# Dense experts: eight tiles per PSUM sum, splits of 1024 columns, two tiles per gelu and gate product, gathers in the output-only stretch

## The chip, the core and the metric

The kernel runs on one core of one Trainium2 chip. The metric is the device time of one execution in microseconds (us). TensorE does the matrix products, VectorE and ScalarE the elementwise work, GpSimd issues the indirect loads (gathers), and SyncE's queue (SP) issues nearly all other transfers; all transfers share 16 DMA engines. In the rows PE is TensorE, PEld its weight load, DVE VectorE, ACT ScalarE, POOL GpSimd, SP SyncE.

## The reference, cut to what matters

One encoder layer on 512 tokens of width 2048. Two mixers (retention, dilated attention) and a projection give x; the change touches only what follows, the PEER layer:

```
h2 = rms_norm(x); q = h2 @ w_query
for each token, 8 heads: top 16 of 16384 experts by two sub-key scores (e1, e2); gates = softmax
a   = h2 . u[expert]                       # 128 chosen experts per token
out = sum over them of gelu(a) * gate * v[expert]
x   = x + out
```

u and v are (16384, 2048) in float32.

## The kernel before, in words

Products keep float32 accuracy by splitting each operand into a high part (a cast on ScalarE) and a low part (a subtraction on VectorE); each product is three matmuls: high x high, high x low, low x high.

The 512 tokens are four blocks of 128. Blocks 0 and 1 are **gathered**: per block (a `Unit`) 128 rows of u, then 128 rows of v are fetched, one row for each token at a time, by an indirect DMA on GpSimd (`gather_issue`, L752), and used on VectorE (`gather_use`, L761 and L770). Three row buffers turn. `tick(anchor, rate)` adds `rate` to a credit; for each whole credit it uses the oldest row if more than two wait, and issues the next gather; its VectorE work is queued behind `anchor`. Block 0's gathers run under the second mixer; block 1's 256 gathers run under the dense experts.

Blocks 2 and 3 (256 tokens, `ND`) are **dense**: all 16384 experts in 128 tiles of 128. For a tile, `expert_in` (L848 to L850, 48 matmuls of 256 columns) makes a = u h2 in PSUM (`psa`), gelu goes to `ge` (L853); `load_u` loads the next tile of u, 1 MB, and splits it in four pieces of 512 columns (L836, L837). The weights of the gates are built earlier as a dense table GD by one-hot products (L906 to L915): in 32 steps of 8 tokens VectorE compares, ScalarE scales by the gate, TensorE multiplies. `weigh` multiplies `ge` by the table (L937) and splits the product (L940, L941). `expert_out` takes v in pieces of two tiles x 512 columns (L955, split at L958 and L959) and sums NV = 4 tiles in PSUM (`psy`, L965 to L967, 24 matmuls of 512 columns a tile), then adds the sum to `yacc` in SBUF (L970), with one tick behind each addition.

In time: 24 tiles of `expert_in` run ahead, 11 while the routing is done and most of the others between the one-hot steps, which carry a tick of 1.2 each. Then come the groups: group g weighs its tiles and runs `expert_in` for those from 24 on, and `expert_out` of group g-1. So there are some groups with output alone and no tick, then 25 groups with both and 8 ticks each, which spread what is left of the 256 gathers evenly, and a last group of output alone with no tick. The compiler's scheduler fixes each engine's order from program order and its own costs; on each engine and each queue that order is then kept. SP's queue holds the loads of u, v and the gate table in one order.

## Time and profile before

| | us |
|---|---|
| time, median of 3 runs | 4723.65 (4723.06 to 4727.6) |
| profiled execution, its own time | 4720.41 |
| its span | 4718.6 |
| TensorE busy in the span | 4278.5 |
| VectorE busy | 3560.2 |
| ScalarE busy | 1999.0 |
| GpSimd busy | 746.5 |

The profiled execution's time is 1.8 us more than its span. A busy matmul is one in the pipeline, so a share of 100% doesn't say that TensorE is at its peak: there the distance between two starts is read. A VectorE operation's duration overlaps the next one's a little: there, too, the distance between starts is what it costs in a row.

### The profile page before, as it was taken

How to read it: one execution, taken by the hardware profiler on the slowest of the kernel's cores; microseconds unless marked ns; L12 is line 12 of the kernel's file. 1: busy time of each engine (PE TensorE's matmuls, PEld its weight loads, DVE VectorE, ACT ScalarE, POOL GpSimd, SP SyncE). 2: the span in 40 equal slices, each digit the busy share in tenths (PEclk: the TensorE clock that was granted, in tenths of full speed). 3: DMA queues.
4: the chain of work that ended last, by engine and by line, in shares of the span. 5: the costliest groups of instructions: out<-in, count | busy, mean ns of one | idle time of the engine just before them, and what ended most of it. 6: DMA issues, size and time to landing. Idle time of an engine off the chain costs nothing.

```text
span 4718.6 us, 58782 instructions
## 1 busy us (share of the span) xinstructions
PE 4278.5 (91%) x21606; PEld 3567.6 (76%) x21606; DVE 3560.2 (75%) x5039; ACT 1999.0 (42%) x3154; POOL 746.5 (16%) x516
## 2 busy tenths in 40 slices
PE   8999989988989999889879987877999999999998
PEld 6888767765767877677668866876788888888887
DVE  7454645546667788577578869887789999999998
ACT  5444545545433333433432332465444434344343
POOL 0000000000001222122122210032012222244232
PEclk9999999999999999899889988988999999999999
DMA  7667666668668889689599873488789999999998
GB/s 242 221 220 232 210 219 205 224 229 274 205 214 301 328 306 342 217 324 336 192 376 388 342 301 136 143 308 341 235 304 364 360 372 369 379 363 362 359 374 300
DMA packets 491744, 1358.81 MB, mean 288 GB/s; under 512 B 47168, under 2 KB 127040, under 8 KB 405952
## 3 DMA queue, kind: packets, MB, share of 16 engines
q1 hardware_dynamic: 414368, 815.99, 49.5%
q0 software_dynamic: 73728, 536.90, 29.7%
q8 instruction: 169, 2.77, 0.2%
q10 hardware_dynamic: 3360, 2.17, 0.1%
q14 instruction: 119, 0.97, 0.1%
HBM read 1290.05 MB, written 64.88 MB: 287 GB/s over the span
## 4 chain that ended last, share of the span: by engine, by line
PE 49%; issue 17%; DMA 15%; DVE 11%; ACT 4%; POOL 3%; SPq 0%; POOLq 0%; ACTq 0%; DVEq 0%
PE gB L146 11%; PE gB L147 10%; PE gB L145 10%; POOL gr L752 3%; PE psy L966 3%; DMA gr<-in_peer_v,eid 3%; DMA wraw<-in_w_in 3%; PE psy L967 3%; PE psy L965 2%; DVE wlo L130 2%; ACT whi L129 2%; PE psa L848 2%; PE psa L850 2%; PE psa L849 2%; DMA vr<-in_peer_v 1%
## 5 line engine op out<-in xcount | busy, mean ns | idle before, releaser
L130 DVE TENSOR_TENSOR wlo<-wraw,whi 128x1024 fp32r<-128x1024 f32 x752 | 916.3, 1222 | 643.6 <-ACT whi L129 627.6
L129 ACT CAST whi<-wraw 128x1024 fp32r<-128x1024 f32 x752 | 788.4, 1050 | 1188.6 <-PE gB L147 910.6
L752 POOL DMA_INDIRECT gr<-in_peer_u,eid x256 | 329.3, 1286 | 2857.6 <-DVE eid L739 1374.8
L770 DVE SCALAR_TENSOR_TENSOR accg<-gr,wg,accg 128x2048 f32<-128x2048 f32 x256 | 600.3, 2345 | 36.0 <-DMA gr<-in_peer_v,eid 29.1
L761 DVE SCALAR_TENSOR_TENSOR gr<-gr,hrow 128x2048 f32<-128x2048 f32 x256 | 583.4, 2283 | 43.4 <-DMA gr<-in_peer_u,eid 43.3
L848 PE MATMUL psa<-rh,uh 128*128 128x256 f32 x2048 | 581.0, 284 | 30.6 <-ACT uh L836 30.6
L850 PE MATMUL psa<-rh,ul 128*128 128x256 f32 x2048 | 580.8, 284 | 14.5 <-DVE ul L837 14.5
L752 POOL DMA_INDIRECT gr<-in_peer_v,eid x256 | 416.9, 1629 | 1083.9 <-DVE accg L770 911.8
L849 PE MATMUL psa<-rl,uh 128*128 128x256 f32 x2048 | 577.8, 282 | 0.0
L958 ACT CAST vh<-vr 128x1024 fp32r<-128x1024 f32 x256 | 269.3, 1052 | 565.3 <-DMA vr<-in_peer_v 270.5
L966 PE MATMUL psy<-vl,wh 128*128 128x512 f32 x1024 | 416.8, 407 | 31.6 <-DVE vl L959 30.2
L848 PEld LDWEIGHTS psa<-rh,uh 128*128 128x128 f32 x2048 | 393.9, 192 | 39.2 <-ACT uh L836 33.8
L836 ACT CAST uh<-ur 128x512 fp32r<-128x512 f32 x512 | 306.9, 619 | 274.1 <-DMA ur<-in_u_feat 132.1
L965 PE MATMUL psy<-vh,wh 128*128 128x512 f32 x1024 | 391.9, 399 | 32.2 <-ACT vh L958 32.0
L967 PE MATMUL psy<-vh,wl 128*128 128x512 f32 x1024 | 407.5, 398 | 0.0
L850 PEld LDWEIGHTS psa<-rh,ul 128*128 128x128 f32 x2048 | 389.9, 191 | 21.5 <-DVE ul L837 17.2
L849 PEld LDWEIGHTS psa<-rl,uh 128*128 128x128 f32 x2048 | 391.2, 191 | 2.8
L146 PE MATMUL gB<-wlo,rh 128*128 128x512 f32 x768 | 317.6, 414 | 49.2 <-DVE wlo L130 48.7
L837 DVE TENSOR_TENSOR ul<-ur,uh 128x512 fp32r<-128x512 f32 x512 | 324.2, 682 | 29.8 <-ACT uh L836 29.4
L959 DVE TENSOR_TENSOR vl<-vr,vh 128x1024 fp32r<-128x1024 f32 x256 | 308.2, 1220 | 37.5 <-ACT vh L958 37.3
L145 PE MATMUL gB<-whi,rh 128*128 128x512 f32 x768 | 308.8, 405 | 27.4 <-ACT rh L566 20.7
L147 PE MATMUL gB<-whi,rl 128*128 128x512 f32 x768 | 310.7, 405 | 0.6 <-DVE rl L567 0.5
(465 smaller groups left out, 8190.6 us busy)
## 6 DMA issues: line engine op xcount, KB each, us to landing
wraw<-in_w_in SPq DMA_DIRECT2D x528, 512.0 KB, 5.1
ur<-in_u_feat SPq DMA_DIRECT2D x128, 1024.0 KB, 8.6
vr<-in_peer_v SPq DMA_DIRECT2D x256, 512.0 KB, 7.7
wraw<-in_w_ret_out SPq DMA_DIRECT2D x64, 512.0 KB, 6.1
wraw<-in_w_out SPq DMA_DIRECT2D x64, 512.0 KB, 6.0
wraw<-in_peer_w_query SPq DMA_DIRECT2D x64, 512.0 KB, 5.2
...
```

The lines of the kernel that those rows point to most:

```text
L129: nc.scalar.copy(whi, raw)
L130: low = nc.vector.tensor_sub(wlo, raw, whi.bitcast(F32))
L145: nc.tensor.matmul(ps[t], ah(k), whi[:, j], start=first, stop=False)
L146: nc.tensor.matmul(ps[t], ah(k), wlo[:, j], start=False, stop=False)
L147: nc.tensor.matmul(ps[t], al(k), whi[:, j], start=False, stop=last)
L752: nc.gpsimd.indirect_dma_start(out=r, out_offset=None, in_=pu if s < P else pv_, in_offset=bass.IndirectOffsetOnAxis(ap=u.eid[:, s % P:s % ...
L761: nc.vector.scalar_tensor_tensor(r, r, 1.0, u.hrow, op0=ALU.mult, op1=ALU.mult, accum_out=u.ag[:, s:s + 1])
L770: nc.vector.scalar_tensor_tensor(u.acc, r, u.wg[:, s - P:s - P + 1], u.acc, op0=ALU.mult, op1=ALU.add)
L848: nc.tensor.matmul(psa[:, :ND], uh[:, cs], chi[k], start=k == 0, stop=False)
L849: nc.tensor.matmul(psa[:, :ND], uh[:, cs], clo[k], start=False, stop=False)
L850: nc.tensor.matmul(psa[:, :ND], ul[:, cs], chi[k], start=False, stop=k == KT - 1)
L966: nc.tensor.matmul(ps[t], wh[:, ts_], vl[:, j], start=False, stop=False)
```

## The change

- `NV` goes from 4 to 8: eight tiles per sum in `psy`, so 16 groups in place of 32. `psy` is now one tile of two banks (both blocks of tokens), and one addition of 1024 columns goes to `yacc` where there were two of 512. A call of `expert_out` does half a chunk: two pieces of v.
- `load_u` loads u in two halves of 1024 columns through three buffers (before: whole, two buffers) and splits each half in one go.
- `psa` holds two tiles; gelu, gate product and split are done on two tiles at once; all `ge` stay in one pool.
- In each one-hot step half of the 8 tokens get comparison and scale in one VectorE operation in place of VectorE and ScalarE; the tick there is 1.0.
- Ticks stand once in each call of `expert_out`, behind the last split of v, and from the first group on: 0.7 each in the groups with output alone ahead of tile 24, then an even spread over the rest but the last group.
- PSUM pools lie on other sides; `psB` is closed before the groups and `psY` takes its banks.

```diff
--- before.py
+++ after.py
@@ -70,7 +70,8 @@
 
     const = ctx.enter_context(tc.tile_pool(name="const", bufs=1))
     dram = ctx.enter_context(tc.tile_pool(name="dram", bufs=1, space=DRAM))
-    psB = ctx.enter_context(tc.tile_pool(name="psB", bufs=4, space=PSUM))
+    back = ctx.enter_context(ExitStack())
+    psB = back.enter_context(tc.tile_pool(name="psB", bufs=4, space=PSUM, side="right"))
     front = ctx.enter_context(ExitStack())
     psA = front.enter_context(tc.tile_pool(name="psA", bufs=4, space=PSUM))
     h_ctx = ExitStack()
@@ -813,7 +814,7 @@
     TB = 64
     NB = ND // TB
     NE = 2
-    NV = 4
+    NV = 8
     NGRP = P // NV
     NPRE = 24
     NFIRST = 11
@@ -826,42 +827,44 @@
 
     def load_u(n):
 
-        ur = pools["d1"].tile([P, D], F32, name="ur", bufs=2)
-        nc.sync.dma_start(ur, I["u_feat"][n])
         U[n] = []
-        for q in range(4):
-            part = ur[:, q * 512:(q + 1) * 512]
-            uh = pools["d1"].tile([P, 512], F32R, name="uh", bufs=5)
-            ul = pools["d1"].tile([P, 512], F32R, name="ul", bufs=5)
-            nc.scalar.copy(uh, part)
-            nc.vector.tensor_sub(ul, part, uh.bitcast(F32))
+        for q in range(2):
+            ur = pools["d1"].tile([P, 1024], F32, name="ur", bufs=3)
+            nc.sync.dma_start(ur, I["u_feat"][n][:, q * 1024:(q + 1) * 1024])
+            uh = pools["d1"].tile([P, 1024], F32R, name="uh", bufs=3)
+            ul = pools["d1"].tile([P, 1024], F32R, name="ul", bufs=3)
+            nc.scalar.copy(uh, ur)
+            nc.vector.tensor_sub(ul, ur, uh.bitcast(F32))
             U[n].append((uh, ul))
 
     def expert_in(n):
 
         if n + 1 < P:
             load_u(n + 1)
-        psa = pools["psE"].tile([P, 512], F32, name="psa")
+        j = n % NE
+        if j == 0:
+            pools["psa"] = pools["psE"].tile([P, NE, ND], F32, name="psa")
+        psa = pools["psa"]
         for k in range(KT):
-            uh, ul = U[n][k // 4]
-            cs = slice(k % 4 * P, (k % 4 + 1) * P)
-            nc.tensor.matmul(psa[:, :ND], uh[:, cs], chi[k], start=k == 0, stop=False)
-            nc.tensor.matmul(psa[:, :ND], uh[:, cs], clo[k], start=False, stop=False)
-            nc.tensor.matmul(psa[:, :ND], ul[:, cs], chi[k], start=False, stop=k == KT - 1)
+            uh, ul = U[n][k // 8]
+            cs = slice(k % 8 * P, (k % 8 + 1) * P)
+            nc.tensor.matmul(psa[:, j], uh[:, cs], chi[k], start=k == 0, stop=False)
+            nc.tensor.matmul(psa[:, j], uh[:, cs], clo[k], start=False, stop=False)
+            nc.tensor.matmul(psa[:, j], ul[:, cs], chi[k], start=False, stop=k == KT - 1)
         del U[n]
-        ge = (pools["pre"] if n < NPRE else pools["d1"]).tile([P, ND], F32, name="ge", bufs=NPRE if n < NPRE else 2)
-        nc.scalar.activation(ge, psa[:, :ND], AF.Gelu)
-        A_out[n] = ge
+        if j == NE - 1:
+            ge = pools["pre"].tile([P, NE, ND], F32, name="ge", bufs=NPRE // NE)
+            nc.scalar.activation(ge, psa, AF.Gelu)
+            A_out[n // NE] = ge
 
     hk_T = dram.tile([3, P, ND], F32, name="hk_T")
-    pre_ctx = ExitStack()
 
     def begin_dense():
         wbuf["ctx"].close()
         front.close()
         pools["psE"] = ctx.enter_context(tc.tile_pool(name="psE", bufs=4, space=PSUM, reuse_waits="tile"))
         pools["d1"] = right.enter_context(tc.tile_pool(name="d1", bufs=2, side="right", reuse_waits="tile"))
-        pools["pre"] = pre_ctx.enter_context(tc.tile_pool(name="pre", bufs=1, side="right", reuse_waits="tile"))
+        pools["pre"] = right.enter_context(tc.tile_pool(name="pre", bufs=1, side="right", reuse_waits="tile"))
         load_u(0)
         for n in range(NFIRST):
             expert_in(n)
@@ -904,77 +907,88 @@
                 oh2 = gb.tile([P, OB, P], F32, name="oh2", bufs=2)
                 oh1 = gb.tile([P, OB, P], F32, name="oh1", bufs=2)
                 nc.vector.tensor_tensor(oh2, cols(e2T), every, op=ALU.is_equal)
-                last = nc.vector.tensor_tensor(oh1, cols(e1T), every, op=ALU.is_equal)
+                last = nc.vector.tensor_tensor(oh1[:, :4], cols(e1T)[:, :4], every[:, :4], op=ALU.is_equal)
                 for q in range(OB // 4):
                     ps = bank("gg")
                     for i in range(4):
                         j = 4 * q + i
-                        nc.scalar.activation(oh1[:, j], oh1[:, j], AF.Copy, scale=gT[:, t0 + j:t0 + j + 1])
+                        col = slice(t0 + j, t0 + j + 1)
+                        if q == 0:
+                            nc.scalar.activation(oh1[:, j], oh1[:, j], AF.Copy, scale=gT[:, col])
+                        else:
+                            nc.vector.tensor_scalar(oh1[:, j], iota, e1T[:, col], gT[:, col], op0=ALU.is_equal,
+                                                    op1=ALU.mult)
                         nc.tensor.matmul(ps[:, i * P:(i + 1) * P], oh2[:, j], oh1[:, j], start=True, stop=True)
                     j0 = o * OB + 4 * q
                     nc.scalar.copy(Gs[:, :, j0:j0 + 4], ps.rearrange("p (t e) -> p e t", t=4))
-                tick(last, 1.2)
+                tick(last, 1.0)
             nc.sync.dma_start(GD[blk], Gs)
         for n in range(NPRE - NLAST, NPRE):
             expert_in(n)
+    back.close()
+    psY = ctx.enter_context(tc.tile_pool(name="psY", bufs=2, space=PSUM, side="right", reuse_waits="tile"))
     d2 = ctx.enter_context(tc.tile_pool(name="d2", bufs=2, reuse_waits="tile"))
 
-    yacc = [d2.tile([P, D], F32, name=f"yacc{t}", bufs=1) for t in range(TG)]
+    yacc = d2.tile([P, TG, D], F32, name="yacc", bufs=1)
     for t in range(TG):
-        nc.sync.dma_start(yacc[t], x1D[2 + t])
+        nc.sync.dma_start(yacc[:, t], x1D[2 + t])
 
     W = {}
 
-    def gate_tile(g):
+    def gate_tile(m):
         Gt = d2.tile([P, NB, NE * TB], F32, name="Gt")
-        nc.sync.dma_start(Gt, GD[:, :, NE * g:NE * (g + 1), :].rearrange("b p e t -> p b (e t)"))
+        nc.sync.dma_start(Gt, GD[:, :, NE * m:NE * (m + 1), :].rearrange("b p e t -> p b (e t)"))
         return Gt
 
-    def weigh(n, Gt):
-        ge = A_out.pop(n)
-        j = n % NE
-        gv = ge.rearrange("p (b t) -> p b t", t=TB)
-        nc.vector.tensor_mul(gv, gv, Gt[:, :, j * TB:(j + 1) * TB])
-        wh = d2.tile([P, ND], F32R, name="wh", bufs=2 * NV)
-        wl = d2.tile([P, ND], F32R, name="wl", bufs=2 * NV)
+    def weigh(m, Gt):
+        ge = A_out.pop(m)
+        gv = ge.rearrange("p j (b t) -> p b j t", t=TB)
+        nc.vector.tensor_mul(gv, gv, Gt.rearrange("p b (j t) -> p b j t", t=TB))
+        wh = d2.tile([P, NE, ND], F32R, name="wh", bufs=7)
+        wl = d2.tile([P, NE, ND], F32R, name="wl", bufs=7)
         nc.scalar.copy(wh, ge)
         nc.vector.tensor_sub(wl, ge, wh.bitcast(F32))
-        W[n] = (wh, wl)
+        W[m] = (wh, wl)
 
     G0 = NPRE // NV
-    left_steps = [(NGRP - 1 - G0) * 4 * TG]
-
-    def expert_out(g, chunks):
-        late = g == NGRP - 1
-        for c in chunks:
-            cs = slice(c * 512, (c + 1) * 512)
-            ps = [bank("psy") for t in range(TG)]
-            for q in range(0, NV, NE):
-                n0 = NV * g + q
-                vr = d2.tile([P, NE, 512], F32, name="vr", bufs=3)
-                nc.sync.dma_start(vr, pv_[n0 * P:(n0 + NE) * P, cs].rearrange("(e p) c -> p e c", p=P))
-                vh = d2.tile([P, NE, 512], F32R, name="vh")
-                vl = d2.tile([P, NE, 512], F32R, name="vl")
-                nc.scalar.copy(vh, vr)
-                nc.vector.tensor_sub(vl, vr, vh.bitcast(F32))
-                for t in range(TG):
-                    ts_ = slice(t * P, (t + 1) * P)
-                    for j in range(NE):
-                        wh, wl = W[n0 + j]
-                        first, last = q + j == 0, q + j == NV - 1
-                        nc.tensor.matmul(ps[t], wh[:, ts_], vh[:, j], start=first, stop=False)
-                        nc.tensor.matmul(ps[t], wh[:, ts_], vl[:, j], start=False, stop=False)
-                        nc.tensor.matmul(ps[t], wl[:, ts_], vh[:, j], start=False, stop=last)
+    early_rate = 0.7
+    left_steps = [(NGRP - 1 - G0) * 8]
+
+    def expert_out(g, i):
+
+        c, half = i // 2, i % 2
+        cs = slice(c * 512, (c + 1) * 512)
+        if half == 0:
+            pools["psy"] = psY.tile([P, TG, 512], F32, name="psy")
+        ps = pools["psy"]
+        for q in range(half * NV // 2, (half + 1) * NV // 2, NE):
+            n0 = NV * g + q
+            vr = d2.tile([P, NE, 512], F32, name="vr", bufs=3)
+            nc.sync.dma_start(vr, pv_[n0 * P:(n0 + NE) * P, cs].rearrange("(e p) c -> p e c", p=P))
+            vh = d2.tile([P, NE, 512], F32R, name="vh")
+            vl = d2.tile([P, NE, 512], F32R, name="vl")
+            nc.scalar.copy(vh, vr)
+            low = nc.vector.tensor_sub(vl, vr, vh.bitcast(F32))
+            wh, wl = W[n0 // NE]
             for t in range(TG):
                 ts_ = slice(t * P, (t + 1) * P)
-                add = nc.vector.tensor_add(yacc[t][:, cs], yacc[t][:, cs], ps[t])
-                if late:
-                    nc.scalar.dma_start(out4[2 + t][:, cs], yacc[t][:, cs])
-                elif g >= G0:
-                    n = (len(gstate["todo"]) + 0.01) / left_steps[0]
-                    left_steps[0] -= 1
-                    tick(add, n)
-        if late:
+                for j in range(NE):
+                    first, last = q + j == 0, q + j == NV - 1
+                    nc.tensor.matmul(ps[:, t], wh[:, j, ts_], vh[:, j], start=first, stop=False)
+                    nc.tensor.matmul(ps[:, t], wh[:, j, ts_], vl[:, j], start=False, stop=False)
+                    nc.tensor.matmul(ps[:, t], wl[:, j, ts_], vh[:, j], start=False, stop=last)
+        if half == 1:
+            nc.vector.tensor_add(yacc[:, :, cs], yacc[:, :, cs], ps)
+            if g == NGRP - 1:
+                for t in range(TG):
+                    nc.scalar.dma_start(out4[2 + t][:, cs], yacc[:, t, cs])
+        if g < G0:
+            tick(low, early_rate)
+        elif g < NGRP - 1:
+            rate = (len(gstate["todo"]) + 0.01) / left_steps[0]
+            left_steps[0] -= 1
+            tick(low, rate)
+        else:
             gather_use(0)
 
     for g in range(NGRP + 1):
@@ -985,11 +999,10 @@
                     Gt = gate_tile(n // NE)
                 if n >= NPRE:
                     expert_in(n)
-                weigh(n, Gt)
+                if n % NE == NE - 1:
+                    weigh(n // NE, Gt)
             if g > 0:
-                expert_out(g - 1, (q,))
-        if NV * (g + 1) == NPRE:
-            pre_ctx.close()
+                expert_out(g - 1, q)
     assert not gstate["todo"]
     gather_use(0)
```

## Rows read from the trace of the kernel before

**Rows 1.** The page's first part: busy us, share, instructions of each engine.
```profile
PE 4278.5 (91%) x21606; PEld 3567.6 (76%) x21606; DVE 3560.2 (75%) x5039; ACT 1999.0 (42%) x3154; POOL 746.5 (16%) x516
```

**Rows 2.** Stretches: length; busy of PE, PEld, DVE, ACT, POOL; granted clock, DMA share, GB/s.
```profile
3075.00:3276.00 201.00, 150.95 (x997) 140.66 (x998) 182.59 (x181) 139.95 (x374) 72.94 (x38) 0.84 0.82 319
...
3304.00:3435.00 131.00, 125.58 (x544) 101.75 (x545) 100.77 (x144) 59.84 (x77) 0.00 (x0) 0.99 0.69 231
...
3460.00:4665.00 1205.00, 1128.70 (x7080) 1009.89 (x7079) 1126.25 (x1284) 492.44 (x783) 350.67 (x213) 0.98 0.96 364
...
4665.00:4718.00 53.00, 40.72 (x151) 31.00 (x149) 38.19 (x33) 11.30 (x12) 7.07 (x5) 0.87 0.72 261
```

**Rows 3.** Order of time on TensorE: start, duration, instruction; twelve starts apart each.
```profile
3800.66 0.28 PE L848 MATMUL psa<-rh,uh 128*128 128x256 f32 x1
...
3802.03 0.28 PE L848 MATMUL psa<-rh,uh 128*128 128x256 f32 x1
...
3803.90 0.39 PE L965 MATMUL psy<-vh,wh 128*128 128x512 f32 x1
...
3806.62 0.39 PE L965 MATMUL psy<-vh,wh 128*128 128x512 f32 x1
```

**Rows 4.** Shorter stretches, columns as in rows 2.
```profile
2700.00:2750.00 50.00, 50.00 (x220) 41.04 (x219) 40.09 (x28) 14.57 (x18) 14.74 (x11) 1.00 1.03 403
...
4040.00:4080.00 40.00, 40.00 (x258) 36.25 (x257) 38.93 (x42) 16.87 (x28) 9.78 (x7) 1.00 1.02 393
...
4220.00:4240.00 20.00, 13.23 (x73) 11.39 (x72) 13.08 (x14) 5.12 (x8) 3.21 (x3) 0.83 0.82 299
```

**Rows 5.** Order of time in the paced stretch, GpSimd and VectorE; brackets: idle before.
```profile
4213.06 5.55 POOL L752 DMA_INDIRECT gr<-in_peer_v,eid  x1 [1.92 <-DVE accg L770]
...
4229.42 2.35 DVE L770 SCALAR_TENSOR_TENSOR accg<-gr,wg,accg 128x2048 f32<-128x2048 f32 x1 [4.70 <-DMA gr<-in_peer_v,eid]
...
4588.98 2.35 DVE L770 SCALAR_TENSOR_TENSOR accg<-gr,wg,accg 128x2048 f32<-128x2048 f32 x1 [3.42 <-DMA gr<-in_peer_v,eid]
```

**Rows 6.** Waits from 3450 to 4650: us in total, times, longest.
```profile
ACT vh L958 <- DMA vr<-in_peer_v: 261.5, 66, 6.7
```

**Rows 7.** Order of time on VectorE in the paced stretch.
```profile
3923.61 0.42 DVE L941 TENSOR_TENSOR wl<-ge,wh 128x256 fp32r<-128x256 f32 x1
3923.95 1.22 DVE L959 TENSOR_TENSOR vl<-vr,vh 128x1024 fp32r<-128x1024 f32 x1
3925.08 2.49 DVE L837 TENSOR_TENSOR ul<-ur,uh 128x512 fp32r<-128x512 f32 x4
3927.49 1.22 DVE L959 TENSOR_TENSOR vl<-vr,vh 128x1024 fp32r<-128x1024 f32 x1
3928.62 0.68 DVE L970 TENSOR_TENSOR yacc<-yacc,psy 128x512 f32<-128x512 f32 x1
3929.22 2.28 DVE L761 SCALAR_TENSOR_TENSOR gr<-gr,hrow 128x2048 f32<-128x2048 f32 x1
```

**Rows 8.** DMA queues from 3450 to 4650: packets, MB, share of 16 engines (q1 SP, q0 GpSimd).
```profile
q1 hardware_dynamic: 92293, 217.12, 49.0%
q0 software_dynamic: 30007, 218.57, 46.9%
```

**Rows 9.** Order of time: a one-hot step on VectorE; six scales and a gather in the mixer.
```profile
3150.14 1.22 DVE L906 TENSOR_TENSOR oh<-hkT,iota 128x1024 f32<-128x1024 f32 x1
3151.28 1.22 DVE L907 TENSOR_TENSOR oh<-hkT,iota 128x1024 f32<-128x1024 f32 x1
3152.41 2.28 DVE L761 SCALAR_TENSOR_TENSOR gr<-gr,hrow 128x2048 f32<-128x2048 f32 x1
...
3154.62 1.22 DVE L906 TENSOR_TENSOR oh<-hkT,iota 128x1024 f32<-128x1024 f32 x1
...
1952.23 1.26 DVE L460 TENSOR_SCALAR P<-P,lt 128x128 f32<-128x128 f32 x6
...
1950.37 2.75 POOL L752 DMA_INDIRECT gr<-in_peer_u,eid  x1 [23.39 <-DVE gr L761]
```

## The prediction

> **What bounds the kernel now.** I read the page first, then the table of stretches, then the order of time inside the long one, its waits and its DMA queues, because a mean over the program says little here: TensorE is busy 91% and VectorE 75% of it [rows 1], and the change touches only the dense experts at its end. Four stretches matter [rows 2]. In the one-hot stretch (3075 to 3276) VectorE has the largest share, 182.6 of 201 us, at a granted clock of 0.84. In the output-only stretch (3304 to 3435) TensorE has 125.6 of 131 us, VectorE 100.8, GpSimd nothing, and the DMA engines stand at 0.69. In the paced stretch (3460 to 4665), which is a quarter of the program, three things are nearly full at once: TensorE 1128.7 and VectorE 1126.3 of 1205 us, DMA 0.96. The tail (4665 to 4718) holds 151 matmuls in 53 us.
>
> The paced stretch has 7080 matmuls; a tile has 48 of "in" and 24 of "out", so that is 98.3 tiles at **12.25 us**. Twelve matmuls of 256 columns start 1.37 us apart and twelve of 512 columns 2.72 us apart [rows 3], so TensorE alone needs 48 x 0.114 + 24 x 0.227 = **10.92 us** a tile. VectorE has 1126.3/98.3 = **11.46 us** a tile. The DMA engines need 0.96 x 12.25 = **11.76 us** a tile if a share of 1.0 is their end. So the order of the floors is transfers, VectorE, TensorE, and what is lost above them is lost in hand-overs: one window of 20 us has 73 matmuls where the pace would give 117 [rows 4], and in it VectorE stood 4.70 us for a gathered row that GpSimd had needed 5.55 us to issue [rows 5]. ScalarE waited 261.5 us for loads of v [rows 6].
>
> **The change part by part.** The sum is made against the profiled execution, 4720.4 us (span 4718.6), which is 3.2 us under the median of the runs, 4723.65.
>
> *Where the gathers go.* There are 256 for the second unit. Before, 32 ticks of 1.2 issue 38 in the one-hot stretch, and 218 are spread over 200 ticks in 25 groups, 100 tiles: 2.18 a tile. After, 32 ticks of 1.0 issue 32, 24 ticks of 0.7 issue 17, and 207 are left for 96 steps of one tile: 2.16 a tile. The early gathers are thus nearly all eaten by the shorter paced stretch; the load of one paced tile doesn't fall. What falls is the number of paced tiles, from 100 to 96: four tiles go from 12.25 us to TensorE's 10.92, **-5 us**. At most -5, and 0 if the light tiles keep the paced rate.
>
> *VectorE in the paced stretch.* Four subtractions of 512 columns take 2.41 us start to start, one operation of 1024 takes 1.13, one addition of 512 takes 0.60 [rows 7]. The additions to yacc go from two of 512 a tile (1.20) to half of one of 1024 (0.57): -0.63. The u splits go from 2.41 to 2 x 1.13: -0.14. The gate products and the splits of w go from two of 256 a tile to one of 512; I price that by spacing at 0.67 against 0.60: -0.07. Together -0.84, so VectorE falls from 11.46 to about 10.6 us a tile, below the transfers. That is where its stall goes; the transfers end last next. Against the change: u comes in two loads of 4 KB a partition in place of one of 8 KB. The SP queue's 92293 packets for 217.12 MB had 49.0% of 16 engines over 1200 us, GpSimd's 30007 for 218.57 MB had 46.9% [rows 8]; solved for bytes and packets that is 0.0074 us a packet, and 128 more packets a tile are 0.06 us. So the floor of transfers is 11.82 us a tile, and the best stretch, 40 us at 393 GB/s against a mean of 364 [rows 2, 4], allows 11.35 for the same bytes (364 x 12.25 / 393). The bounds are 11.35 and 12.25 (nothing gained); I take 11.85, near the mean service time, since only a stretch of another stage shows more, 403 GB/s over 50 us [rows 4]. 96 x (12.25 - 11.85) = **-38 us**, between 0 and -86.
>
> *One-hot stretch.* A step is 1.14 + 1.13 for two comparisons and 2.21 for a gather, 4.48 us [rows 9], and 4.92 with 1.2 gathers. After: 1.14 + 0.60 + four operations on 128x128 + one gather. The nearest row is a scale of 128x128, six of which take 1.26 us, 0.21 each [rows 9]: 0.84, together 4.79. That is -0.13 a step, -4 over 32, and 12 tiles x 0.14 of u splits, -2: **-6 us**. If the new operation, which does two things with two scalars, costs as much as a split of 256 columns, 0.34 [rows 7], the step is 5.31 and the stretch loses 10; if ScalarE's relief (half of its scales go) also takes away VectorE's idle time, 18 us, the stretch gains up to 15.
>
> *Output-only stretch.* It holds 16 tiles in place of 20, and the tail 8 in place of 4; 24 tiles of 5.44 us either way, so no gain by itself. The gathers come in: 0.7 x 2.21 = 1.55 us a tile to 2.27 (v) + 0.57 + 0.60, which is 5.0 of 5.44 us on VectorE, 92%. The cover holds but is thin, and the first group now weighs pairs before it can begin. I take **+4 us**, between 0 and +10. The issue on GpSimd is free there, as its row says. If the cover went, 17 gathers of 2.21 us would show as 38 us.
>
> *Tail.* 151 matmuls of 0.227 us are 34 of its 53 us; a longer last group has more of TensorE's work to lay over the last gathers. I take 0, between -10 and +5.
>
> *What else moves.* The one tick a step stands behind the second v split in place of behind each addition; the rows it uses are three gathers back as before. The gate's activation waits for two tiles, but its product is needed only a group later. The u ring holds a tile and a half in place of two; the second half's load waits in SP's queue for a split, with v loads behind it. The load it waits for is needed over two tiles later, so I take nothing; were it late, its price is in the bound 12.25.
>
> Sum: 4720.4 - 5 - 38 - 6 + 4 + 0 = **4675 us**.
>
> **A page weighed.** A gather that was issued just ahead of six scales of 128x128 lasted 2.75 us on GpSimd, nearly to their end, and one issued ahead of back-to-back splits lasted 5.55 us [rows 5, 9]. The Trainium skill, "SBUF — State Buffer", section "Who interferes with whom", says that VectorE's fast scalar operations lock GpSimd out of a port that it needs to write descriptors, and that operations with two SBUF inputs hold up GpSimd's reads. The trace agrees with both so far. By it the four new scalar operations of a step could hold a gather up by their 0.84 us, and the sum would be 27 us higher, 4702, if each delay reached VectorE. That would need a row with no time to spare: in the one-hot stretch a row is used three steps after it was issued, 3 x 4.8 us, so I leave it out of the sum.
>
> **The rivals.**
> *The pace stays (0.22).* If late gathers and not full engines set the 12.25, a VectorE with slack only waits longer. For it: the window with 73 matmuls is of this kind [rows 4, 5]. Against it: VectorE is 93% busy and TensorE's own waits on it are many. Price: only -5 - 6 + 4 = 4713 us, at the edge of a measurable gain.
> In a sentence apart: the Trainium skill, "DMA: Bandwidth & Descriptors", section "Specifications", gives about 358 GB/s from HBM to one core; by that the paced stretch, at 364, is at its end and the time is 4713. The trace differs: 50 us at 403 GB/s [rows 4].
> *TensorE becomes the bound (0.10).* The transfers reach 393 GB/s throughout: 11.35 us a tile, -86 in place of -38: 4627 us. For it: those 40 us have TensorE full [rows 4]. Against: it is the best stretch that I found.
> *Late gathers, slower (0.12).* In a step the two or three uses (2.21 us each) now run in a row behind the v split, and the splits behind them form one train with hardly an addition between, during which the last gather's issue hangs (5.55 us). When the row is late VectorE stops at accg in the paced stretch, then TensorE. Price: (117 - 73) / 5.88 a us = 7.5 us an event. The time is over that of before from 6 more events on (45 / 7.5); 18 more, which is a fifth of the steps, give 4675 + 135 = 4810. For it: such waits exist. Against: only four of over 2 us are there now, the first and the last in [rows 5].
> *A gather held up by the new scalar operations (0.03).* 32 steps x 0.84 us in the one-hot stretch are 27 us: 4702. For it: the 2.75 us [rows 9]. Against: the three steps in hand.
>
> **How the numbers follow.** Forecast 0.53, pace stays 0.22, TensorE bound 0.10, late gathers 0.12, the lock 0.03. A measurement tells 0.2%, 9.4 us: faster is below 4714, slower above 4733. Faster holds the forecast, the TensorE case, the lock and half of the first rival: 0.77; same 0.11; slower 0.12. The forecast's own range is 4640 to 4710 (11.5 to 12.2 us a tile). Taking in the first rival whole, the TensorE case and the mild end of the slow one gives 4622 to 4728.
>
> **What would show it.** In the new profile: paced tiles at 11.85 us with DMA at 0.98 or more and VectorE at 90% or less; 256 additions to yacc become 64; gathers between the first and the last output-only tile; the one-hot step at 4.8 us. I am wrong if the DMA share stays at 0.96 with the pace, if VectorE's waits for gathered rows grow beyond 15 us, or if the output-only stretch loses more than 10 us.

## The result and the profile after

The changed kernel takes **4646.46 us** (median of 4 runs, 4638.18 to 4658.38) against 4725.62 us for the kernel before in the same runs (4723.06 to 4732.96): a ratio of 0.9832, 95% interval [0.9806, 0.9858]. That is 79 us less. The forecast was 4675 us, which is 45 us under the profiled execution of before and 49 under its median. The profiled execution took 4638.18 us, its span 4636.4.

The first part of its page (as rows 1):

```profile
PE 4230.3 (91%) x21606; PEld 3542.0 (76%) x21606; DVE 3462.9 (75%) x4591; ACT 1913.0 (41%) x2642; POOL 792.9 (17%) x516
```

The stretches of the changed kernel, columns as in rows 2, are the one-hot stretch, the boundary behind it, the output-only stretch, the paced stretch and the tail:

```profile
3080.00:3286.00 206.00, 138.96 (x997) 132.35 (x995) 177.44 (x267) 98.82 (x216) 50.00 (x30) 0.85 0.72 273
3286.00:3317.00 31.00, 17.31 (x118) 16.63 (x118) 8.97 (x11) 4.94 (x7) 1.68 (x1) 0.83 0.92 350
...
3317.00:3440.00 123.00, 112.70 (x472) 88.53 (x473) 99.93 (x98) 48.55 (x53) 19.61 (x13) 0.96 0.89 315
...
3460.00:4570.00 1110.00, 1101.36 (x7105) 1003.82 (x7104) 1031.83 (x833) 457.32 (x493) 386.15 (x207) 1.00 1.01 392
...
4573.00:4636.00 63.00, 53.05 (x219) 41.99 (x218) 36.92 (x28) 17.85 (x18) 3.93 (x3) 0.93 0.63 222
```

The paced stretch holds the gain. It has 7105 matmuls, 72 a tile, so 98.7 tiles at **11.25 us** where [rows 2] had 12.25. TensorE is busy 1101 of 1110 us, so it is now the engine that ends last. VectorE has 1031.83/98.7 = 10.46 us a tile (11.46 before; over 3500 to 4500 alone, the stretch of the table below, it is 10.58), and the DMA engines moved 392 GB/s (364 before). Taken in stretches of 50 us, the pace is nearly even. Here are one of the best of them and the only one with a deep dip:

```profile
4390.00:4440.00 50.00, 50.00 (x337) 46.13 (x336) 45.37 (x33) 20.65 (x22) 18.46 (x10) 1.00 1.03 405
...
3940.00:3990.00 50.00, 44.06 (x269) 39.31 (x270) 48.02 (x35) 18.44 (x20) 19.21 (x10) 0.97 0.99 382
```

Waits from 3460 to 4570 (us in total, times, longest), the answer to rows 5 and 6:

```profile
DVE vl L971 <- ACT vh L970: 36.5, 34, 3.8
DVE accg L771 <- DMA gr<-in_peer_v,eid: 10.3, 17, 1.5
DVE gr L762 <- DMA gr<-in_peer_u,eid: 8.3, 8, 2.5
...
ACT vh L970 <- DMA vr<-in_peer_v: 111.5, 55, 5.3
```

ScalarE's wait for v fell from 261.5 us [rows 6] to 111.5. VectorE waits 18.6 us for gathered rows (15.8 before), but in 25 pieces, the longest of 2.5 us, where there were eight of up to 4.7 us [rows 5]. Windows of 20 us like that with 73 matmuls [rows 4] are gone: the least, in the one dip, has 94.

The DMA queues from 3450 to 4570 (packets, MB, share of 16 engines), the answer to rows 8:

```profile
q1 hardware_dynamic: 108372, 221.02, 53.2%
q0 software_dynamic: 29760, 216.68, 47.3%
```

More packets carry about the same bytes as in rows 8, in 1120 us where rows 8 needed 1200. The share of 0.96 was thus not the end of the transfers, and 1.0 is not either (1.03 above). Where their end lies, no run here shows.

A one-hot step on VectorE (start, duration, instruction), the answer to rows 9:

```profile
3271.38 1.22 DVE L909 TENSOR_TENSOR oh<-hkT,iota 128x1024 f32<-128x1024 f32 x1
3272.52 0.68 DVE L910 TENSOR_TENSOR oh<-hkT,iota 128x512 f32<-128x512 f32 x1
3273.12 1.11 DVE L919 TENSOR_SCALAR oh<-iota,hkT,hkT 128x128 f32<-128x128 f32 x4
3274.14 2.29 DVE L762 SCALAR_TENSOR_TENSOR gr<-gr,hrow 128x2048 f32<-128x2048 f32 x1
...
3276.36 1.22 DVE L909 TENSOR_TENSOR oh<-hkT,iota 128x1024 f32<-128x1024 f32 x1
```

The four new operations take 1.02 us from start to start (3273.12 to 3274.14), 0.256 each. The step, from one L909 to the next, is 4.98 us.

**Where the 82 us between the two profiled spans are.** The lengths are those of the stretches here and in rows 2, whose marks are good to 1 or 2 us. The first mark comes 5 us later (3080 against 3075); 3 of them stand already at the first "in" matmul of all (2995.6 against 2992.8), and x3, with the same code up to there, has 2991.4. The one-hot stretch is 5 us longer (206, 201), the boundary 3 us (31, 28). From the first output matmul to the last "in" matmul there are 1256 us in place of 1361, and the tail has 63 in place of 53.

What a stretch lost is its length less its matmuls by the spacing of rows 3. The output-only stretch has 435 "out" matmuls and 37 "in", 103 us of work in 123, so it lost 20; before it had 531 and 13, 122 in 131, so it lost 9. The tail took over 68 matmuls (216 "out" and 3 "in" against 142 and 9), 16 us that only moved; it lost 20 us before and 14 after. So: +5 +5 +3, output-only +11, tail -6, and what is left, -100, is in the paced stretch: -82 in all.

### The profile page after: what moved, and what is told of

The parts are those of the page before. It is cut to its first block, busy times and chain, and to the rows that moved or that the text cites. A ratio compares the mean times of both kernels' runs of the same rounds, so it can differ in the third digit from the quotient of the medians.

```text
span 4636.4 us, 57934 instructions
## 1 busy us (share of the span) xinstructions
PE 4230.3 (91%) x21606; PEld 3542.0 (76%) x21606; DVE 3462.9 (75%) x4591; ACT 1913.0 (41%) x2642; POOL 792.9 (17%) x516
## 4 chain that ended last, share of the span: by engine, by line
PE 44%; issue 20%; DMA 16%; DVE 12%; POOL 4%; ACT 4%; SPq 0%; POOLq 0%; ACTq 0%; DVEq 0%
PE gB L147 10%; PE gB L148 10%; PE gB L146 9%; POOL gr L753 4%; DMA wraw<-in_w_in 4%; DVE wlo L131 2%; DMA wraw<-in_w_out 2%; PE psa L853 2%; PE psa L851 2%; PE psa L852 2%; PE psy L978 2%; ACT whi L130 2%; PE psy L979 2%; PE psy L977 2%; DVE accg L771 2%
## 5 line engine op out<-in xcount | busy, mean ns | idle before, releaser
L753 POOL DMA_INDIRECT gr<-in_peer_u,eid x256 | 356.6, 1393 | 2776.8 <-DVE eid L740 1532.2
L753 POOL DMA_INDIRECT gr<-in_peer_v,eid x256 | 436.1, 1704 | 1009.0 <-DVE accg L771 849.4
L836 ACT CAST uh<-ur 128x1024 fp32r<-128x1024 f32 x256 | 269.0, 1052 | 474.2 <-DMA ur<-in_u_feat 307.0
L978 PE MATMUL psy<-vl,wh 128*128 128x512 f32 x1024 | 405.9, 396 | 17.6 <-DVE vl L971 17.4
L977 PE MATMUL psy<-vh,wh 128*128 128x512 f32 x1024 | 403.5, 394 | 7.5 <-ACT vh L970 7.5
L837 DVE TENSOR_TENSOR ul<-ur,uh 128x1024 fp32r<-128x1024 f32 x256 | 310.9, 1218 | 59.3 <-ACT uh L836 59.2
L146 PE MATMUL gB<-whi,rh 128*128 128x512 f32 x768 | 308.8, 405 | 29.7 <-ACT rh L567 20.8
```

The source lines that it names most:

```text
L146: nc.tensor.matmul(ps[t], ah(k), whi[:, j], start=first, stop=False)
L753: nc.gpsimd.indirect_dma_start(out=r, out_offset=None, in_=pu if s < P else pv_, in_offset=bass.IndirectOffsetOnAxis(ap=u.eid[:, s % P:s % ...
L978: nc.tensor.matmul(ps[:, t], wh[:, j, ts_], vl[:, j], start=False, stop=False)
```

## The experiments

**The theories.** V: VectorE's amount of work set the pace of the paced stretch, and taking 0.9 us a tile off it let TensorE set the pace. T: not the amount but the order counts (one tick a step behind a split, halves of u, fewer operations). D: the transfers hold the pace. Later, K: there is a knee, a load of VectorE past which more is lost than the excess. Against K stand S (only the sum of work counts, and the fuller engine sets the pace) and G (what x10 loses comes from its gathers, not from VectorE).

Twelve kernels, each timed beside the kernel before on its chip; the three groups of runs have medians of 4725.7, 4740.2 and 4730.5 us for the kernel before, so the ratios are what is compared. "Tile" is worked out from the stretch of 3500 to 4500 us of each profile: 1000 x 72 / matmuls; "VectorE" is its busy time there a tile. x2 and x14 are probes only: they leave out 384 of the 2048 columns of that part of the output. The two lines of before and after (columns as in rows 2):

```profile
3500.00:4500.00 1000.00, 934.61 (x5853) 835.27 (x5852) 931.70 (x1073) 407.93 (x652) 279.19 (x175) 0.98 0.97 366
...
3500.00:4500.00 1000.00, 991.36 (x6398) 903.55 (x6397) 939.95 (x762) 410.14 (x443) 354.61 (x191) 1.00 1.02 398
```

| kernel | us | ratio to before, 95% | tile us | VectorE us |
|---|---|---|---|---|
| before | | 1 | 12.30 | 11.46 |
| after | 4646.5 | 0.9832 [0.9806, 0.9858] | 11.25 | 10.58 |
| x1 extra subtraction | 4755.2 | 1.0058 [1.0036, 1.0080] | 12.17 | 11.61 |
| x2 before, shorter uses | 4645.0 | 0.9836 [0.9807, 0.9865] | 11.60 | 10.65 |
| x3 four tiles a sum | 4629.1 | 0.9798 [0.9776, 0.9820] | 11.14 | 10.95 |
| x4 one-hot part undone | 4617.4 | 0.9760 [0.9734, 0.9787] | 11.27 | 10.60 |
| x7 x3 and x4 | 4600.6 | 0.9714 [0.9690, 0.9738] | 11.15 | 10.95 |
| x8 x3, tick behind the addition | 4748.0 | 1.0016 [0.9997, 1.0034] | 12.21 | 11.10 |
| x9 x3, u whole | 4631.2 | 0.9774 [0.9749, 0.9799] | 11.29 | 11.05 |
| x10 x3, no early gathers | 4734.8 | 0.9988 [0.9972, 1.0005] | 12.11 | 11.26 |
| x11 x3, small extra subtraction | 4687.2 | 0.9897 [0.9875, 0.9919] | 11.62 | 11.23 |
| x12 x10, third buffer for vh, vl | 4777.6 | 1.0090 [1.0064, 1.0116] | 12.77 | 11.25 |
| x13 before, tick behind the split | 4714.5 | 0.9971 [0.9949, 0.9992] | 12.21 | 11.44 |
| x14 x2 and x13 | 4629.4 | 0.9788 [0.9766, 0.9810] | 11.27 | 10.60 |

### x1: the relief given back

```
+            if G0 <= g < NGRP - 1 and q == half * NV // 2:
+                nc.vector.tensor_sub(vl, vr, vh.bitcast(F32))
             low = nc.vector.tensor_sub(vl, vr, vh.bitcast(F32))
```

> The changed kernel with the first v split of every paced step written twice: one more subtraction of 1024 columns a tile on VectorE, 1.13 us, nothing else. Theory V (VectorE's amount of work set the pace before, and its relief let TensorE set it): VectorE goes from 10.56 to 11.7 us a tile, so the paced stretch returns from 11.2 to about 12 to 12.5 us a tile; 96 tiles, 4646 + 80 to 125 = 4725 to 4770 us, TensorE's share of the stretch falls from 0.99 to about 0.92. Theory T (what counted was the order: one tick a step, halves of u, fewer hand-overs): VectorE's extra work falls into idle time, within 20 us of 4646 us.

Measured 4755 us, within V's range. The stretch of 3500 to 4500 (columns as in rows 2):

```profile
3500.00:4500.00 1000.00, 933.77 (x5917) 839.39 (x5916) 954.42 (x789) 379.15 (x411) 362.34 (x175) 0.98 0.97 366
```

One more VectorE operation a tile, no byte more to move, and the DMA engines fall back to 366 GB/s and 0.97, the numbers of the kernel before. So 364 GB/s was what the pace asked for, not what the engines could give. D falls with this, and so does T's "within 20 us of 4646 us": the amount of work counts.

### x2: the old kernel with lighter uses

```
-nc.vector.scalar_tensor_tensor(u.acc, r, u.wg[:, s - P:s - P + 1], u.acc, op0=ALU.mult, op1=ALU.add)
+nc.vector.scalar_tensor_tensor(u.acc[:, :w], r[:, :w], u.wg[:, s - P:s - P + 1], u.acc[:, :w], ...)   # w = 1664 of 2048
...   # the use of a row of u in the same way
```

> The kernel before, with each use of a gathered row in the paced stretch and after it on 1664 of its 2048 columns (384 columns of that part of the output are left out); the gathers, the splits, the additions and the ticks stay. VectorE loses 384/2048 of 2.21 us in 2.18 uses a tile, 0.90 us a tile, about what the change took off. Theory V: the paced stretch goes from 12.25 to 11.1 to 11.4 us a tile, 100 tiles, 4725 - 85 to 115 = 4610 to 4640 us, with the DMA engines near 400 GB/s. Theory T: the order is that of before, so the time stays within 25 us of 4725. Theory D (transfers of whole u rows and their order hold the pace at 364 GB/s): the same, with VectorE's share falling to 0.85.

Measured 4645 us, just past V's 4640, and as fast as the changed kernel.

```profile
3500.00:4500.00 1000.00, 971.68 (x6208) 877.63 (x6207) 917.86 (x1136) 445.18 (x692) 295.26 (x187) 1.00 1.01 391
```

The old u loads and the old order reach 391 GB/s once VectorE has 10.65 us a tile. But the pace is 11.60, not the 11.25 that the changed kernel has at 10.58: about a third of a microsecond a tile belongs to something other than the amount.

### x3: four tiles a sum in the changed kernel

```
-    NV = 8
+    NV = 4
-        c, half = i // 2, i % 2
+        c = i
-        if half == 1:
-            nc.vector.tensor_add(yacc[:, :, cs], yacc[:, :, cs], ps)
+        nc.vector.tensor_add(yacc[:, :, cs], yacc[:, :, cs], ps)
```

> The changed kernel with four expert tiles in a PSUM sum in place of eight: one chunk of 512 columns a step is finished, with one addition of 1024 columns to yacc in every step in place of every second one. VectorE has 0.57 us a tile more, 11.13. Theory V: it comes close to TensorE's 11.2, so 0 to 0.5 us a tile is lost in 100 tiles: 4646 to 4696 us, less up to 10 us for a tail of four tiles in place of eight; I expect +20. Theory T: no loss in the paced stretch, 4636 to 4646.

Measured 4629 us: not the 20 us more that I expected, but 17 less. T's 4636 is nearer.

```profile
3500.00:4500.00 1000.00, 998.04 (x6463) 911.35 (x6462) 983.26 (x804) 423.44 (x450) 351.55 (x186) 1.00 1.02 397
```

VectorE took back 0.37 us a tile (half an addition of 1024 columns is 0.57, but its 207 paced gathers are spread over 100 tiles in place of 96, which gives some 0.19 back), is busy 983 of 1000 us, and still TensorE has 998. So the headline of the change, eight tiles a sum, brings nothing once the rest is in place: VectorE's 10.95 is under TensorE's 11.14, and that is enough. The 11.14 is TensorE's own time: without a break its "in" matmuls start 1.41/12 = 0.118 us apart here,

```profile
3799.81 0.28 PE L851 MATMUL psa<-rh,uh 128*128 128x256 f32 x1
...
3801.22 0.28 PE L851 MATMUL psa<-rh,uh 128*128 128x256 f32 x1
```

and 48 x 0.118 + 24 x 0.227 is 11.1 us. From the first output matmul to the end the profile has 1304.5 us against 1319.1; 10 of these 14.6 us are the pace (0.11 x 96), the rest lies in the stretches around it. The intervals of x3 and of the changed kernel overlap, so a gain from four tiles alone is likely, not certain.

### x4: the one-hot part undone

```
-                last = nc.vector.tensor_tensor(oh1[:, :4], cols(e1T)[:, :4], every[:, :4], op=ALU.is_equal)
+                last = nc.vector.tensor_tensor(oh1, cols(e1T), every, op=ALU.is_equal)
...
-                        if q == 0:
-                            nc.scalar.activation(oh1[:, j], oh1[:, j], AF.Copy, scale=gT[:, col])
-                        else:
-                            nc.vector.tensor_scalar(oh1[:, j], iota, e1T[:, col], gT[:, col], ...)
+                        nc.scalar.activation(oh1[:, j], oh1[:, j], AF.Copy, scale=gT[:, col])
```

> The changed kernel with the one-hot part as before (one comparison of eight tokens, all eight scales on ScalarE), but with the new rate of one gather a step. If the four new VectorE operations (0.257 us each) in place of half a comparison lengthened the stretch, a step goes from 4.98 to 4.48 us: 32 x 0.5 = 16 us less, 4630 us. If ScalarE's longer queue (eight scales, and the u splits behind them) holds the step, or if the stretch is held by the write of the gates and the loads, it stays within 5 us of 4646.

Measured 4617 us, an interval clear of the changed kernel's. A step in its order of time on VectorE:

```profile
3247.65 1.22 DVE L909 TENSOR_TENSOR oh<-hkT,iota 128x1024 f32<-128x1024 f32 x1
3248.79 1.22 DVE L910 TENSOR_TENSOR oh<-hkT,iota 128x1024 f32<-128x1024 f32 x1
3249.93 2.28 DVE L762 SCALAR_TENSOR_TENSOR gr<-gr,hrow 128x2048 f32<-128x2048 f32 x1
...
3252.14 1.22 DVE L909 TENSOR_TENSOR oh<-hkT,iota 128x1024 f32<-128x1024 f32 x1
```

```profile
3081.00:3270.00 189.00, 150.32 (x995) 139.72 (x995) 166.04 (x145) 134.68 (x346) 59.04 (x31) 0.83 0.80 303
```

4.49 us a step (3247.65 to 3252.14), and 189 us for the stretch in place of 206. ScalarE has all eight scales again, 134.68 of 189 us, and is not in the way. In the changed kernel work was moved from an engine with room to the one that sets the end of this stretch. The medians say 29 us, the stretch explains 17, the boundary behind it 3; the rest is within what the runs of x4 differ by (4600 to 4634).

### x7: both, the best version

> Four expert tiles a sum and the one-hot part as before, at one gather a step, both in the changed kernel. If the two gains lie in different stretches they add: the marks of the two runs gave -15 us from the first output matmul on and -20 us up to it, so 4646 - 35 = 4611 us, with the one-hot stretch at 189 us, the paced tile at 11.15 and the tail at 35 us. If the later start of the gathers (VectorE fuller in the one-hot stretch) is paid back later, 4620 to 4630.

Four tiles a sum (the edit of x3) and the one-hot part as before (that of x4). Measured **4600.6 us**, ratio 0.9714: the two gains add (0.9798 and 0.9760 against 0.9832 would give 0.9726), and this is faster than both kernels. Its stretches (one-hot, then first output matmul to the last "in" matmul):

```profile
3084.00:3273.00 189.00, 147.83 (x995) 137.55 (x993) 165.88 (x145) 134.49 (x345) 58.61 (x31) 0.86 0.81 305
...
3301.00:4564.00 1263.00, 1251.73 (x7802) 1125.95 (x7803) 1229.37 (x1019) 528.69 (x563) 423.24 (x223) 1.00 1.00 386
```

In the second one TensorE is busy 99% and VectorE 97%.

### x8: the tick behind the addition

```
-        nc.vector.tensor_add(yacc[:, :, cs], yacc[:, :, cs], ps)
+        low = nc.vector.tensor_add(yacc[:, :, cs], yacc[:, :, cs], ps)
```

> The kernel with four expert tiles a sum, with the tick of every step behind its addition to yacc (as in the kernel before) in place of behind its last v split. Theory V (only the amount of VectorE's work counts): 4629 us within 10. Theory T, that the place of the tick counts: the issue of the next gather and the uses wait for TensorE's last matmul of the step, so VectorE stands while TensorE works and the paced tile goes from 11.14 towards the 11.60 of the kernel before with shorter uses: +20 to +45, 4650 to 4675.

Measured 4748 us: T's direction was right, and the loss is far over its 4650 to 4675. One word is added, and the whole gain of the change is gone.

```profile
3500.00:4500.00 1000.00, 946.31 (x5895) 842.76 (x5894) 908.50 (x749) 382.72 (x413) 344.57 (x171) 0.98 0.96 362
```

Waits in that stretch:

```profile
DVE yacc L978 <- PE psy L977: 23.2, 35, 2.3
...
PE psy L975 <- ACT vh L968: 24.3, 16, 3.0
PE psy L976 <- DVE vl L969: 24.2, 32, 2.8
```

The addition waits for the step's last matmul (35 times; in x3 11 times, 3.9 us in all), the two gather uses stand behind it in a row, and the splits for TensorE's next matmuls stand behind those. A step of x8 on VectorE, in order of time:

```profile
3806.91 1.22 DVE L978 TENSOR_TENSOR yacc<-yacc,psy 128x1024 f32<-128x1024 f32 x1 [0.88 <-PE psy L977]
3808.05 2.28 DVE L762 SCALAR_TENSOR_TENSOR gr<-gr,hrow 128x2048 f32<-128x2048 f32 x1
...
3810.26 2.29 DVE L762 SCALAR_TENSOR_TENSOR gr<-gr,hrow 128x2048 f32<-128x2048 f32 x1
...
3812.47 1.22 DVE L969 TENSOR_TENSOR vl<-vr,vh 128x1024 fp32r<-128x1024 f32 x1
```

With the tick behind the split the uses lie in the time in which TensorE still works on the step. VectorE is busy only 91% here: its waits, not its work alone, fill the tile. That the tick's place costs this is shown by the edit; the way there is read from the waits.

### x9: u whole again

```
-        for q in range(2):
-            ur = pools["d1"].tile([P, 1024], F32, name="ur", bufs=3)
-            nc.sync.dma_start(ur, I["u_feat"][n][:, q * 1024:(q + 1) * 1024])
+        ur = pools["d1"].tile([P, D], F32, name="ur", bufs=2)
+        nc.sync.dma_start(ur, I["u_feat"][n])
```

> The kernel with four expert tiles a sum, with u loaded whole (8 KB a partition, two buffers) and split in four operations of 512 columns, as before. VectorE has 0.15 us a tile more, 11.1, and ScalarE two operations more. Theory V: VectorE is then at TensorE's 11.14, so 0 to +15 us: 4629 to 4645. Theory T, that the halves count: a v load stands behind a whole u load, ScalarE's vh comes late, and the paced tile goes to 11.5 to 11.6: +35 to +45, 4665 to 4675, with VectorE waiting for vh some 60 us in 1000.

Measured 4631 us: no loss. The tile is 11.29 (x3 11.14), but the ratio is not worse than that of x3. The halves of u and their splits of 1024 columns are worth nothing that this measurement tells, and the 0.35 us of x2 is not theirs.

### x10: no gathers in the output-only stretch

```
-    early_rate = 0.7
+    early_rate = 0.0
```

> The kernel with four expert tiles a sum, without gathers in the output-only stretch: 17 more gathers in its 100 paced tiles, 0.17 x 2.21 = 0.37 us a tile more on VectorE, 11.3. Theory V: that is over TensorE's 11.14, so the paced tile goes to 11.3 to 11.6: 4629 + 16 to 46 = 4645 to 4675 us, less up to 5 for a lighter output-only stretch. If VectorE still had room, as its idle time of 2 in 100 says it has not, within 10 us of 4629.

Measured 4735 us: 17 more gathers in the paced stretch cost some 90 us by the ratios (0.9988 against 0.9798), about twice the upper end of my range. The stretch of 3500 to 4500, then two of 50 us, early and later:

```profile
3500.00:4500.00 1000.00, 942.91 (x5945) 846.92 (x5944) 929.68 (x774) 382.27 (x413) 295.36 (x182) 0.99 0.99 377
...
3590.00:3640.00 50.00, 48.36 (x317) 44.09 (x316) 48.61 (x46) 19.99 (x23) 15.82 (x10) 1.00 1.02 397
...
3890.00:3940.00 50.00, 45.11 (x284) 40.63 (x283) 43.24 (x41) 17.82 (x20) 14.04 (x9) 0.97 0.97 362
```

At first VectorE is full and TensorE nearly keeps its pace; some 300 us later TensorE, VectorE and the DMA engines are all below their best at once. VectorE, with 11.26 us a tile, does not even get those done in 11.3: the tile is 12.11. A part of the excess is TensorE's clock. Here TensorE stood 4.22 us for a v split; in 3 us behind that it started 8 matmuls at a granted clock of 0.50 (1.2 GHz), and then 14 in 3 us at 1.00 (2.4 GHz):

```profile
3912.88 0.50 PE L976 MATMUL psy<-vl,wh 128*128 128x512 f32 x1 [4.22 <-DVE vl L969]
...
3913.50:3916.50 3.00, 3.00 (x8) 2.34 (x7) 3.00 (x4) 0.00 (x0) 0.06 (x1) 0.50 1.01 386
3916.80:3919.80 3.00, 3.00 (x14) 2.47 (x14) 1.58 (x2) 1.06 (x1) 2.70 (x2) 1.00 0.56 209
```

A tile of x10 is 0.97 us longer than one of x3. TensorE stands for 0.67 of them and is busy 0.30 us longer, which bounds what the clock costs.

### x11: just over the knee, with VectorE's work alone

```
+            if G0 <= g < NGRP - 1 and q == 0:
+                nc.vector.tensor_sub(vl[:, 0, :256], vr[:, 0, :256], vh.bitcast(F32)[:, 0, :256])
             low = nc.vector.tensor_sub(vl, vr, vh.bitcast(F32))
```

> The kernel with four expert tiles a sum, with one more subtraction of 256 columns on VectorE in every paced step (a quarter of a v split, written twice): 0.34 us a tile, so VectorE goes from 10.95 to 11.29 us against TensorE's 11.14; no transfer and no gather is added. Theory K (a knee: as soon as VectorE's work is over TensorE's, VectorE falls behind, the few buffers between them run empty, and each waits for the other): the paced tile falls to 12.0 to 12.2 us, 4629 + 85 to 105 = 4715 to 4735 us, after a start at 11.1, with VectorE's share falling below 0.95. Theory S (the sum alone: the engine with more work sets the pace): 11.3 to 11.5, 4645 to 4665. Theory G (the 105 us of the run without early gathers came from gathers, not from VectorE): within 10 of 4629.

Measured 4687 us, 20 to 30 us from both K's and S's range; G's "within 10 of 4629" is out. One stretch of 50 us in each state:

```profile
3840.00:3890.00 50.00, 49.98 (x327) 45.57 (x326) 49.96 (x51) 21.49 (x23) 14.91 (x9) 1.00 1.01 388
...
4190.00:4240.00 50.00, 43.15 (x269) 38.48 (x267) 42.23 (x34) 18.64 (x20) 13.25 (x9) 0.93 0.90 336
```

Up to 3890 it holds the full pace with VectorE at 99%, later it falls into dips and comes out again. So there is a knee near TensorE's 11.14 us (x9, at 11.05, is no slower than x3), and past it more is lost than the excess (11.23 of work gives 11.62), but it is no step to 12.1. x10, with the same VectorE work but 2.20 gathers a tile (182 issues in 82.6 tiles) against 2.04 here (176 in 86.1), is much worse: VectorE's sum is not the only thing that counts past the knee.

### x12: a third buffer for the halves of v

```
-            vh = d2.tile([P, NE, 512], F32R, name="vh")
-            vl = d2.tile([P, NE, 512], F32R, name="vl")
+            vh = d2.tile([P, NE, 512], F32R, name="vh", bufs=3)
+            vl = d2.tile([P, NE, 512], F32R, name="vl", bufs=3)
```

> Four expert tiles a sum, no gathers in the output-only stretch, and three buffers in place of two for each half of v (vh, vl), with five in place of seven for wh and wl to make room. Theory K: a third buffer lets VectorE and ScalarE work ahead over a train of gather uses, so part of the 12.1 us a tile comes back, to 11.4 to 11.6: 4735 - 50 to 80 = 4655 to 4685 us. If the hand-over that costs is another (u's halves, or the gate product), within 15 of 4735.

Measured 4778 us, slower than x10 (1.0090 against 0.9988): a third buffer for vh and vl did not bring the time past the knee back. What ScalarE waits for in 3500 to 4500, in x12:

```profile
ACT vh L968 <- DMA vr<-in_peer_v: 445.3, 114, 12.7
```

In x10:

```profile
ACT vh L968 <- DMA vr<-in_peer_v: 207.8, 67, 9.9
```

In x3:

```profile
ACT vh L968 <- DMA vr<-in_peer_v: 49.7, 29, 3.8
```

It is the loads of v that come late. SP's own waits in x10 name two candidates (SPq is SP's queue, L833 the load of u, L965 that of v):

```profile
SPq L833 <- DVE ul L837: 616.4, 164, 9.5
...
SPq L965 <- DVE vl L969: 148.5, 162, 9.2
```

One candidate is that a u load waits in SP's queue until a u split has freed its buffer, with the v loads waiting behind it; in x3 the u loads wait 424.4 us. The trace speaks against it: of the 164 v loads in this stretch of x10, 162 had a v split on VectorE as the last thing that they waited for, the split that freed one of the three buffers vr. (And in x8, with a tile as slow, the u loads wait less than in x3, 263.5 us.) The chain that ended last in x10 from 3890 to 3940 is 37.8% loads of v, and shows the round:

```profile
3895.99 1.15 DVE vl L969
3897.15 11.21 DMA vr<-in_peer_v
...
3911.61 1.23 DVE vl L969
```

A v split frees a buffer, the load into it lands 11.21 us later, and only then can ScalarE cast it and VectorE split it, so a late VectorE makes its own next v late. This is read from the waits and was not tried (more than three buffers vr would try it). x12 also has smaller wh and wl rings (five in place of seven), so it is not a clean test of the third buffer alone.

### x13 and x14: the tick's place in the old kernel

```
-                    tick(add, n)
+                    tick(low, n)      # low: the chunk's last v split
```

> The kernel before with one thing changed: both ticks of a chunk stand behind its last v split in place of behind the two additions. Theory K: VectorE still has 11.46 us of work against TensorE's 11.14, so it stays behind: within 15 of 4725. Theory T (the place of the tick is what the change gained): 11.2 to 11.6 us a tile, 4620 to 4660.

> The kernel before with the ticks behind the last v split and each use of a gathered row in the paced stretch on 1664 of its 2048 columns (384 columns of that part of the output left out): both conditions, in the old sizes of everything else. Theory K, with the tick's place as the second condition: the paced tile goes from the 11.60 of the shorter uses alone to 11.15 to 11.25: 4645 - 35 to 45 = 4600 to 4610 us. If only the amount of work counts and 11.60 has another cause (whole u loads, more and smaller operations): within 10 of 4645.

x13 measured 4715 us, x14 4629 us. Their stretches, x13 first:

```profile
3500.00:4500.00 1000.00, 937.02 (x5898) 843.22 (x5897) 936.82 (x1076) 408.60 (x656) 244.11 (x177) 0.98 0.98 369
```

```profile
3500.00:4500.00 1000.00, 991.36 (x6391) 903.65 (x6389) 941.25 (x1160) 438.76 (x709) 225.16 (x192) 0.99 1.02 400
```

In the old kernel the tick's place alone is worth 0.3%, as K had it: VectorE, at 11.44 us, is past the knee anyway. With the lighter uses it takes the tile from 11.60 to 11.27 us, the pace of the changed kernel, at 400 GB/s and with whole u loads, sums of four tiles, gelu by single tiles and no early gathers. The time stayed 20 us above the top of my 4600 to 4610, though the pace came out almost as expected (11.15 to 11.25, measured 11.27). Of the rest, 7 us lie ahead of the stretch: its first output matmul came at 3312 us, that of x2 at 3305, on a chip on which the kernel before takes 4730.5 us in place of 4725.7.

## Why the prediction came out as it did

**Right in direction and in what VectorE's relief does, wrong in what ends last after it.** The paced stretch was named as the place, VectorE's relief as the cause. The step that failed is "So the floor of transfers is 11.82 us a tile", on the condition "if a share of 1.0 is their end", and from it "I take 11.85, near the mean service time". Measured: 11.25 us a tile at a mean share of 1.01, with 1.03 and 405 GB/s in the best stretches, and TensorE, not the transfers, ends last. The term is 96 x 1.0 = 96 us where 38 was taken, and even the bound of 86 was a little short. x1 and x2 show the reading error: the transfers' rate followed the pace (366 GB/s with one VectorE operation more, 391 with lighter uses in the old kernel), so a share of 0.96 said nothing of a limit. The row that was right was the best short stretch, 393 GB/s with TensorE full [rows 4], which the prediction had in hand and gave 0.10.

**Luck.** The time is inside the forecast's own range of 4640 to 4710, but the pace is not inside its 11.5 to 12.2 us a tile. With the other terms as forecast, the paced stretch alone would have given some 4618 us. The one-hot and output-only stretches, the boundary and a later start lost some 20 us more than forecast and brought the time back into the range. Two of the three signs of being wrong came about as well: waits for rows of over 15 us, and over 10 us lost in the output-only stretch.

**TensorE's floor** was a little low too. The 10.92 us that "TensorE alone needs" took 0.114 us for an "in" matmul from twelve starts in rows 3; in an unbroken run they start 0.118 us apart (x3), which makes 11.1 us a tile.

**VectorE's relief.** Forecast 0.84 us a tile, measured 0.88 (11.46 to 10.58, table): right. But not all its parts were needed. The sums of eight tiles, the largest part of it by the forecast (0.63 with the merged addition), can be undone at no loss (x3), and from there so can the halves of u (x9).

**The tick.** "The one tick a step stands behind the second v split in place of behind each addition; the rows it uses are three gathers back as before" was priced at nothing. In the four-tile form of the new kernel, with VectorE at 11 us, the tick's place is worth 1.07 us a tile (x8 against x3), all of the gain. In the old kernel it is worth 0.09 alone and 0.33 with the lighter uses (x13, x14), and two thirds of the gain came without it (x2, with VectorE at 10.65). So the gain has two conditions: VectorE's work under TensorE's 11.14 us, and, the more the less room that leaves, gather uses that lie ahead of the addition that waits for TensorE. The prediction had the first. That room decides how much the second counts is argued, since x2 and x8 differ in more than that. Whether the eight-tile kernel would lose as much by the tick's place was not tried.

**The early gathers.** "the load of one paced tile doesn't fall" is right as a comparison with the kernel before (2.18 and 2.16 a tile), and the output-only stretch paid for them, +11 us by the account above where +4 was taken and +10 was the bound. x10, without them, lost only 6 us there: 393 "out" and 25 "in" matmuls, 92 us of work, in the 98 us from 3334 to 3432. Without them, though, the four-tile kernel goes over the knee (x10, some 90 us). Whether the eight-tile kernel, with 0.37 us more room, needs them was not tried.

**One-hot stretch.** Forecast -6 us, measured +5: the wrong sign. The new operation was priced by the scale of 128x128, 0.21 us [rows 9]; it takes 0.256, so the step is 4.98 and not 4.79. That is 6 us in 32 steps. The rest is VectorE waiting for ScalarE's cast of u, 20.8 us in the stretch where it was 1.1; its wait for rows fell from 16.3 to 5.8. The larger error was to compare with the step at 1.2 gathers: the lower rate alone brings the step to 4.49 (x4), and the moved scales give 16 us of that back.

**The rivals.**

*TensorE becomes the bound* (0.10) came about: 11.25 us a tile, under its 11.35. Its 4627 us was not reached since the one-hot and the output-only stretch lost what it did not count.

The Trainium skill, "DMA: Bandwidth & Descriptors", section "Specifications", with its 358 GB/s from HBM to one core, differs from the trace, which has 392 GB/s over 1110 us; the same skill says in "Perfetto Trace Analysis", section "Roofline", that this share holds with both cores of a pair at work and that a core alone can draw more, up to the some 435 GB/s of its 16 DMA engines. The trace agrees with that: 405 GB/s in the best stretches, on one core.

*The pace stays* did not come about.

*Late gathers, slower* did not: VectorE's waits for rows are 18.6 us, over the 15 named as a sign, but none of them long enough to empty TensorE. Nor are late rows what slows x8, x10 and x12: VectorE waits 4 to 9 us for rows there (3500 to 4500), while TensorE stands for its v splits (44.6 us in x10). What the rival had right is the train: in x8 the uses in a row hold those splits up.

*A gather held up by the new scalar operations*: GpSimd's issues in the one-hot stretch take 50.00/30 = 1.67 us with them and 59.04/31 = 1.90 without (x4); no delay is seen. The Trainium skill, "SBUF — State Buffer", section "Who interferes with whom", tells of a lock: a VectorE operation in a two-port mode and GpSimd keep each other out of the ports that they share. These rows show nothing lost to it.

**Open.** Why a tile takes 12.1 to 12.2 us when VectorE's work is 11.1 to 11.3 (x8, x10). TensorE's lower clock after a stand is a part of it (at most 0.30 of 0.97 us in x10). More depth for vh and vl did not help (x12, not a clean test); the three buffers vr are the next candidate.
